# Summing a late scale and shift on VectorE, and reordering squares, constant products and weight pieces around three norms of a two-layer trunk

## The chip, the core and the metric

The kernel runs on one core of a Trainium2 chip. The metric is the device time of one execution in microseconds (us), the median of several runs; a profiled execution gives the trace. The engines are TensorE (PE in the profile; its weight loads are PEld), VectorE (DVE), ScalarE (ACT), GpSimd (POOL) and SyncE (SP, which issues the loads of weights). Each engine takes its instructions in the order in which they are written; they meet by semaphores.

## What is computed

A trunk of two layers, with 256 tokens of 1024 values in float32. Layer 0 mixes tokens by chunkwise retention and has a dense SwiGLU; layer 1 mixes by attention with forget gates against shared keys and values, and has a SwiGLU of 8 experts, two for each token. Ahead of each of these stands an RMS norm, whose scale and shift (and the gate behind) come from a product of a conditioning vector with a matrix.

```python
def reference(x, c, ada_w, ada_b, norm_g, ...):
    c_act = jax.nn.silu(c)
    h = x
    for l in range(DEPTH):                                   # DEPTH = 2, N_A = 1
        sh1, sc1, g1, sh2, sc2, g2 = jnp.split(c_act @ ada_w[l] + ada_b[l], 6, axis=-1)
        if l == N_A:
            kv_sh, kv_sc = jnp.split(c_act @ kv_ada_w + kv_ada_b, 2, axis=-1)
            hn_kv = modulate(rmsnorm(h, kv_norm_g), kv_sh, kv_sc)
            shared = fox_shared_kv(hn_kv, fox_w_kv, fox_w_f, fox_b_f)
        a = modulate(rmsnorm(h, norm_g[l, 0]), sh1, sc1)
        if l < N_A:
            mix = retention(a, ret_w_in[l], ret_w_o[l])
        else:
            mix = forgetting_attention(a, fox_w_qg[l - N_A], fox_w_o[l - N_A], *shared)
        h = h + g1[:, None, :] * mix
        m = modulate(rmsnorm(h, norm_g[l, 1]), sh2, sc2)
        ff = swiglu(m, ...) if l % 2 == 0 else moe_swiglu(m, ...)
        h = h + g2[:, None, :] * ff
    f_sh, f_sc = jnp.split(c_act @ final_ada_w + final_ada_b, 2, axis=-1)
    return modulate(rmsnorm(h, final_norm_g), f_sh, f_sc)
```

## The kernel before

The residual stream lies transposed in SBUF as `hT` (128 x 8 x 256: eight blocks of 128 features, 256 tokens). A product in float32 is made of three passes over halves: each factor is split into a high part that TensorE takes at full rate and a residue, and hi x hi, hi x lo and lo x hi are added in PSUM (`PASSES`). The high part of a weight, `whi`, is a cast on ACT (line 153); the residue `wlo` is a subtraction on DVE (recorded at line 184, or where else a list of late steps is run).

**The stream.** All weights pass through one `Stream`. An item is a block of 1 MB, `raw`, which SP loads into one of four buffers; it is worked off in two halves of 128x1024. For a weight, a half gives `whi` and `wlo`, of which six pairs exist. An item with a "use" is no weight: it is a block of a matrix whose product with the conditioning vector is wanted (a constant product). DVE multiplies its rows with the vector and sums them into a tile `adaacc` (lines 257 and 259, 128x1024); eight such steps make one of the vectors (g1, sh2, sc2, ...), and then PE transposes the sum (`pc`, line 268), ACT adds it up (line 273) and DVE adds the bias (line 275). Weights and "use" items stand mixed in one list, and `half()` hands out the next made pair, makes up to three further steps ahead (`fill`), and calls `tick()`, which lets waiting side work go on one step. So the order in which ACT and DVE get casts, residues, constant products and the rest is the order in which these calls are written and the list is laid out.

**The opening.** The first norm needs its scale and shift (sc1, sh1) before the first projection. Each comes in two halves, n = 0 and n = 1. For each half PE multiplies 16 blocks into a bank `prow` (line 306), ACT copies it (line 321), and PE turns it into a column `pcol` (line 317). The half n = 1 comes in between the first retention projections: `pa` (line 572), then `prow`, `pcol`, `pq` (line 724). `shift(n)` makes the high part `ah` (ACT) and the residue `al` (DVE) of the modulated input.

**The norms.** `out_acc` (line 588) adds the last projection of a mixer into four banks `acc`, block by block; two blocks later DVE updates `hT` (line 594) and ACT squares it (line 495), and `norm.sum` sums the squares of earlier blocks over features on PE, with one column as the result (`st`, line 501). So the `st` products stand between the `acc` products. Then `finish`: the root on ACT (`nv`), a Newton step and a diagonal `dg` on DVE, its broadcast `rb` on PE (line 520). `modulate` makes `mt` on DVE (line 529), the high part (`mh`, `kh`, `qh`) on ACT (line 532) and the residue (`ml`, `kl`, `ql`) on DVE (line 535). Norm 1 stands ahead of the SwiGLU of layer 0, norm 2 ahead of keys, values and queries of layer 1, norm 3 ahead of the experts. At norm 1 the next products are gate and up (`pg`, `pu`), 11 pieces each, at norm 2 the keys (`pk`), four pieces; the first piece takes two halves pass by pass (line 557), the others half by half (line 564). Behind norm 3 come the logits of the router, a choice of two experts per token and a gather by products (`pcum`, `P`, `pxe`, line 1227).

## Time and profile before

| what | value |
|---|---|
| median of 3 runs | 1609.03 us (1606.09 to 1609.97) |
| profiled execution, its own time | 1610.43 us |
| its span in the trace | 1608.3 us |
| mean granted clock of TensorE | 0.984 |
| PE busy | 1568.3 us |
| DVE busy | 1388.3 us |
| ACT busy | 1101.7 us |
| POOL busy | 8.7 us |

Busy times are sums over the span; an engine's idle time matters only where the engine that sets the pace waits for it. The experts fill the trace from about 640 us on. The opening, the retention, norm 1 (about 230 to 255 us), the SwiGLU, norm 2 (437 to 452 us), the attention and norm 3 (590 to 625 us) lie before.

### The profile page before, as it was taken

What the parts mean: (1) busy time and instruction counts of PE and PEld (TensorE: products, weight loads), DVE (VectorE), ACT (ScalarE), POOL (GpSimd) and SP (SyncE); (2) the same over time, 40 slices, a digit from 0 to 9 for tenths busy, and PEclk for the clock granted to TensorE, in tenths of its full rate; (3) what the DMA queues carried; (4) which work ended last, traced back from release to release, by engine and by line L of the source; (5) the groups of instructions that cost most, each with busy time, mean ns of one, the idle gap of its engine ahead of it and who ended that gap; (6) DMA issues with size and microseconds to landing.
All of it is one profiled execution on the core that took longest, in us unless ns stands there. A gap on an engine that the chain in (4) does not pass through costs nothing. (4 is left out here: it accounts for less than half of the span.)

```text
span 1608.3 us, 23189 instructions
## 1 busy us (share of the span) xinstructions
PE 1568.3 (98%) x8799; PEld 1345.0 (84%) x8799; DVE 1388.3 (86%) x1649; ACT 1101.7 (68%) x1515; POOL 8.7 (1%) x19
## 2 busy tenths in 40 slices
PE   7999999999999998999999999999999999999996
PEld 5888899999988887888888888888888888888884
DVE  3889878888797977989989989989989988988977
ACT  3444546544475758777887787888778788778774
POOL 0000000000000000000000000000000000000000
PEclk9999988999999998999999999999999999999998
DMA  9888786999868346999999999999999999999990
GB/s 357 296 308 284 288 288 223 351 334 350 301 250 287 132 140 246 372 374 375 354 342 374 351 375 379 357 342 371 351 387 369 358 343 362 357 387 361 362 369 28
DMA packets 182020, 516.02 MB, mean 321 GB/s; under 512 B 8192, under 2 KB 51504, under 8 KB 181904
## 3 DMA queue, kind: packets, MB, share of 16 engines
q1 hardware_dynamic: 180576, 510.82, 85.8%
q0 software_dynamic: 1120, 3.58, 0.6%
q8 instruction: 71, 1.16, 0.3%
q14 instruction: 45, 0.37, 0.1%
q10 hardware_dynamic: 208, 0.08, 0.0%
HBM read 513.40 MB, written 1.05 MB: 320 GB/s over the span
## 5 line engine op out<-in xcount | busy, mean ns | idle before, releaser
L184 DVE TENSOR_TENSOR wlo<-raw,whi 128x1024 fp32r<-128x1024 f32 x830 | 968.9, 1218 | 74.2 <-ACT whi L153 69.7
L153 ACT CAST whi<-raw 128x1024 fp32r<-128x1024 f32 x842 | 863.3, 1053 | 202.0 <-PE yd L572 54.4
L572 PE MATMUL pgu<-whi,xeh 128*128 128x512 f32 x896 | 354.7, 396 | 0.1
L572 PE MATMUL pgu<-wlo,xeh 128*128 128x512 f32 x896 | 349.8, 390 | 0.8 <-DVE wlo L184 0.8
L572 PE MATMUL pgu<-whi,xel 128*128 128x512 f32 x896 | 349.4, 390 | 0.0
L572 PEld LDWEIGHTS pgu<-whi,xel 128*128 128x128 f32 x896 | 168.4, 188 | 36.0
L572 PEld LDWEIGHTS pgu<-wlo,xeh 128*128 128x128 f32 x896 | 168.8, 188 | 33.9 <-DVE wlo L184 1.4
L572 PEld LDWEIGHTS pgu<-whi,xeh 128*128 128x128 f32 x896 | 168.6, 188 | 33.3 <-ACT whi L153 0.5
L572 PE MATMUL yd<-wlo,ehh 128*128 128x512 f32 x448 | 174.5, 390 | 1.2 <-DVE wlo L184 1.2
L572 PE MATMUL yd<-whi,ehh 128*128 128x512 f32 x448 | 174.4, 389 | 0.0
L572 PE MATMUL yd<-whi,ehl 128*128 128x512 f32 x448 | 174.3, 389 | 0.0
L259 DVE SCALAR_TENSOR_TENSOR adaacc<-raw,csil,adaacc 128x1024 f32<-128x1024 f32 x98 | 125.6, 1282 | 1.9
L572 PEld LDWEIGHTS yd<-wlo,ehh 128*128 128x128 f32 x448 | 84.1, 188 | 19.5 <-DVE wlo L184 2.1
L572 PEld LDWEIGHTS yd<-whi,ehh 128*128 128x128 f32 x448 | 84.1, 188 | 17.5
L572 PEld LDWEIGHTS yd<-whi,ehl 128*128 128x128 f32 x448 | 84.1, 188 | 17.4
L213 DVE TENSOR_TENSOR ehl<-pTe,ehh 128x512 fp32r<-128x512 f32 x56 | 38.7, 690 | 38.0 <-ACT ehh L212 37.9
L1315 ACT ACTIVATE ehd<-pgu 128x512 f32<-128x512 f32 x56 | 33.5, 600 | 30.9 <-PE pgu L572 30.9
L572 PE MATMUL pa<-whi,ah 128*128 128x512 f32 x128 | 50.8, 397 | 1.5 <-ACT whi L153 1.5
L212 ACT CAST ehh<-pTe 128x512 fp32r<-128x512 f32 x56 | 32.9, 587 | 28.3 <-PE pTe L1250 28.3
L572 PE MATMUL pa<-wlo,ah 128*128 128x512 f32 x128 | 50.0, 391 | 0.8 <-DVE wlo L690 0.8
L572 PE MATMUL pa<-whi,al 128*128 128x512 f32 x128 | 50.3, 393 | 0.0
L588 PE MATMUL acc<-hh,whi 128*128 128x256 f32 x176 | 49.0, 279 | 0.0
(376 smaller groups left out, 1982.9 us busy)
## 6 DMA issues: line engine op xcount, KB each, us to landing
raw<-in_moe_w_gate_dram SPq DMA_DIRECT2D x112, 1024.0 KB, 7.3
raw<-in_moe_w_up_dram SPq DMA_DIRECT2D x112, 1024.0 KB, 7.2
raw<-in_moe_w_down_dram SPq DMA_DIRECT2D x112, 1024.0 KB, 7.3
raw<-in_ada_w_dram SPq DMA_DIRECT2D x48, 1024.0 KB, 7.2
raw<-in_ret_w_in_dram SPq DMA_DIRECT2D x22, 1024.0 KB, 7.8
raw<-in_ffn_w_gate_dram SPq DMA_DIRECT2D x11, 1024.0 KB, 6.6
raw<-in_ffn_w_up_dram SPq DMA_DIRECT2D x11, 1024.0 KB, 6.9
raw<-in_ffn_w_down_dram SPq DMA_DIRECT2D x11, 1024.0 KB, 7.0
```

The lines of the kernel that those rows point to most:

```text
L153: act.copy(hi, part)
L184: f()
L212: act.copy(hi, src)
L213: vec.tensor_tensor(lo, src, hi.bitcast(F32), op=OP.subtract)
L259: vec.scalar_tensor_tensor(acc, raw[:, kt % 2, :], csil[:, kt:kt + 1], acc, op0=OP.mult, op1=OP.add)
L572: mm(dst, xs[b][:, kt0 + k, t * 128:t * 128 + 128], w[a][:, k, :], start=(first and k == 0 and i == 0), stop=(last and k == nk - 1 and i = ...
L588: mm(acc[nt // 2][:, nt % 2, :], w[a][:, k, nt % 4 * 128:nt % 4 * 128 + 128], xs[b][:, k, :], start=(first and nt % 2 == 0 and k == 0 and ...
L1315: act.activation(hd, pd, AF.Silu)
```

## The change

Five things change.

- **Opening.** The half n = 1 of scale and shift is summed by DVE into `late_acc`, eight operations of 128x512 for each, instead of 16 products on PE and a copy on ACT; the column products read that tile. `shift(0)` is made in two parts, with one step of the stream behind each, and one `prepare()` goes.
- **Constant products.** In the stretches of the list from `wr[-3]` to `wf_[1]` and from `wf_[-3]` to `wx[1]`, which are worked off around norms 1 and 2, the weights come first and the "use" items after them.
- **Squares.** GpSimd adds squares in pairs: 0 and 1; 2 and 3, then that to the first; 4 and 5. PE sums four tiles (0, 4, 6, 7) in place of eight, and all of them after the last `acc` product. Five small products into a bank `idle` are added: one ahead of the sum, two ahead of `rb`, two after it.
- **First pieces.** The first two pieces (`pg` and `pu`; keys 0 and 1) go together in `proj_b2`: four halves at once, 32 products for each of three passes. The first two calls of `half` may still make "use" steps; the ticks come after the passes.
- **Norm 3.** `out_acc` of layer 1 makes two halves of the experts' weights ahead of the norm, where before they were made behind it.

```diff
--- before.py
+++ after.py
@@ -173,13 +173,14 @@
                 steps -= 1
             return later
 
-        def half(self, steps=3):
+        def half(self, steps=3, beside=True, spare=None):
 
             while not self.made:
                 self.start()
             w = self.made.pop(0)
-            later = self.fill(self.spare, steps)
-            tick()
+            later = self.fill(self.spare if spare is None else spare, steps)
+            if beside:
+                tick()
             for f in later:
                 f()
             return w
@@ -301,7 +302,15 @@
         src, off, pitch, _ = ada_src(0, name)
 
         def use(raw, s, h):
-            if h == 0:
+            if n:
+                acc = late_acc[:, 512 * (name == "sh1"):][:, 0:512]
+                for k in (2 * h, 2 * h + 1):
+                    kt = 4 * s + k
+                    if kt == 0:
+                        vec.tensor_scalar(acc, raw[:, k, :], csil[:, 0:1], None, op0=OP.mult)
+                    else:
+                        vec.scalar_tensor_tensor(acc, raw[:, k, :], csil[:, kt:kt + 1], acc, op0=OP.mult, op1=OP.add)
+            elif h == 0:
                 for k in range(4):
                     mm(prow[32 * k:32 * k + 32, :], csp[:, 4 * s + k, :], raw[:, k, :], start=(s == 0),
                        stop=(s == 1), skip_group_check=True)
@@ -313,12 +322,14 @@
 
         bias = ada_src(0, name)[3]
         i = (8 if name == "sh1" else 0) + 4 * n
+        src = late_acc[:, 512 * (name == "sh1"):] if n else rows_sb
         for m in range(4):
-            mm(pcol[:, i + m:i + m + 1], rows_sb[:, m * 128:(m + 1) * 128], ones[:, 0:1], start=True, stop=True)
+            mm(pcol[:, i + m:i + m + 1], src[:, m * 128:(m + 1) * 128], ones[:, 0:1], start=True, stop=True)
         vec.tensor_tensor(t[:, n * 4:n * 4 + 4], pcol[:, i:i + 4], bias[:, n * 4:n * 4 + 4], op=OP.add)
 
     def first_col(name, n, t):
-        act.copy(rows_sb, prow)
+        if n == 0:
+            act.copy(rows_sb, prow)
         turn_col(name, n, t)
 
     ADA = ("sh1", "sc1", "g1", "sh2", "sc2", "g2")
@@ -441,6 +452,10 @@
         + rows(final_ada_w, 0, 2 * D, "fshift", row_bcast(final_ada_b, 0, D), 0.0, None)
         + rows(final_ada_w, D, 2 * D, "fscale", row_bcast(final_ada_b, D, D), 1.0,
                row_bcast(final_norm_g, 0, D)), 0, 70)
+    for a, b in ((wr[-3], wf_[1]), (wf_[-3], wx[1])):
+        lo, hi = (next(i for i, it in enumerate(stream.items) if it is w) for w in (a, b))
+        part = stream.items[lo:hi + 1]
+        stream.items[lo:hi + 1] = [it for it in part if "use" not in it] + [it for it in part if "use" in it]
     for i in range(16, 20):
         stream.items[i]["behind"] = i - 4
     chunks = [(e, j, min(2, EJ - j)) for e in range(NE) for j in range(0, EJ, 2)]
@@ -494,18 +509,22 @@
             sq = self.p.tile([128, S], F32, tag="mt", bufs=8, name="sq")
             act.activation(sq, hT[:, kt, :], AF.Square)
             self.sq.append(sq)
-
-        def sum(self, upto=KT):
-            while self.n < min(upto, len(self.sq)):
+            for a, b in {1: ((0, 1),), 3: ((2, 3), (0, 2)), 5: ((4, 5),)}.get(kt, ()):
+                nc.gpsimd.tensor_tensor(self.sq[a], self.sq[a], self.sq[b], op=OP.add)
+
+        def sum(self):
+            for i in (0, 4, 6, 7):
                 for t in range(TT):
-                    mm(self.st[:, t:t + 1], self.sq[self.n][:, t * 128:(t + 1) * 128], invd,
-                       start=(self.n == 0 and t == 0), stop=(self.n == KT - 1), skip_group_check=True)
-                self.n += 1
+                    mm(self.st[:, t:t + 1], self.sq[i][:, t * 128:(t + 1) * 128], invd,
+                       start=(i + t == 0), stop=(i == 7), skip_group_check=True)
 
         def finish(self, fillers=(gap, gap)):
             if self.sq:
+                busy(1)
                 self.sum()
             fillers[0]()
+            if self.sq:
+                busy(2)
             p = self.p
             v = self.v
             act.activation(v, self.st, AF.Sqrt, bias=epsc)
@@ -519,6 +538,8 @@
             self.rb = bank([128, S], name="rb", tag="at")
             mm(self.rb, ones, dg.rearrange("p t k -> p (t k)"), start=True, stop=True)
             fillers[1]()
+            if self.sq:
+                busy(2)
 
         def modulate(self, g, sh, hi, lo=None):
 
@@ -547,16 +568,20 @@
 
     PASSES = ((0, 0), (1, 0), (0, 1))
 
-    def proj_b(dst, xs, first=False):
-
-        if first:
-            w = [stream.half(), stream.half()]
-            for i, (a, b) in enumerate(PASSES):
-                for kt in range(KT):
-                    for j in range(2):
-                        mm(dst[:, j, :], w[j][a][:, kt, :], xs[b][:, kt, :], start=(kt + i + j == 0),
-                           stop=(i == 2 and kt == KT - 1), skip_group_check=True)
-            return
+    def proj_b2(dsts, xs):
+
+        w = [stream.half(3 if j < 2 else 0, False) for j in range(4)]
+        for i, (a, b) in enumerate(PASSES):
+            for kt in range(KT):
+                for j in range(4):
+                    mm(dsts[j // 2][:, j % 2, :], w[j][a][:, kt, :], xs[b][:, kt, :], start=(kt + i + j % 2 == 0),
+                       stop=(i == 2 and kt == KT - 1), skip_group_check=True)
+            tick()
+            if i:
+                tick()
+
+    def proj_b(dst, xs):
+
         for j in range(2):
             w = stream.half()
             for i, (a, b) in enumerate(PASSES):
@@ -582,7 +607,7 @@
 
         for nt in range(KT):
             if nt % 4 == 0:
-                w = stream.half(0 if last else 3)
+                w = stream.half(3) if not last else stream.half(2 if nt == 0 else 0, spare=1)
             for k in range(nk):
                 for i, (a, b) in enumerate(PASSES):
                     mm(acc[nt // 2][:, nt % 2, :], w[a][:, k, nt % 4 * 128:nt % 4 * 128 + 128], xs[b][:, k, :],
@@ -594,7 +619,6 @@
                         vec.scalar_tensor_tensor(hT[:, m, :], acc[m // 2][:, m % 2, :], gcol[:, m:m + 1],
                                                  hT[:, m, :], op0=OP.mult, op1=OP.add)
                         norm.square(m)
-                norm.sum(nt - 2)
 
     def accs():
         return [bank([128, 2, S], name=f"acc{i}") for i in range(4)]
@@ -634,6 +658,7 @@
             vec.tensor_copy(hT[:, kt:kt + 2, :], px)
         else:
             act.copy(hT[:, kt:kt + 2, :], px)
+    late_acc = ada_acc()
     prow, pcol = bank([128, 512], name="prow", tag="at"), bank([128, 16], name="pcol", tag="at")
     stream.start()
     stream.start()
@@ -660,10 +685,10 @@
                 mts.append(t)
                 vec.scalar_tensor_tensor(t, hT[:, kt, :], G[:, kt:kt + 1], rb_sb, op0=OP.mult, op1=OP.mult)
 
-        def shift(n):
-            for kt in range(n * 4, n * 4 + 4):
+        def shift(n, halves=(0, 4)):
+            for kt in range(n * 4 + halves[0], n * 4 + halves[1]):
                 act.activation(ah[:, kt, :], mts[kt], AF.Identity, bias=sh[:, kt:kt + 1])
-            for kt in range(n * 4, n * 4 + 4):
+            for kt in range(n * 4 + halves[0], n * 4 + halves[1]):
                 vec.scalar_tensor_tensor(al[:, kt, :], mts[kt], sh[:, kt:kt + 1], ah[:, kt, :].bitcast(F32),
                                          op0=OP.add, op1=OP.subtract)
 
@@ -678,7 +703,16 @@
         busy(1)
         first_col("sh1", 0, sh)
         busy(3)
-        shift(0)
+        shift(0, (0, 2))
+        los = []
+        stream.step(los)
+        for f in los:
+            f()
+        shift(0, (2, 4))
+        los = []
+        stream.step(los)
+        for f in los:
+            f()
         nc.gpsimd.tensor_copy(keeppad[:, 0:4], sh[:, 0:4])
 
         def prepare():
@@ -739,7 +773,6 @@
         pv0 = [bank([128, 512], name="pa") for _ in range(TT)]
         pg0 = [bank([128, 512], name="pa", tag="at") for _ in range(TT)]
         prepare()
-        prepare()
         tok0(pv0, 0)
         prepare()
         tok0(pg0, 0)
@@ -749,7 +782,6 @@
         qk0(pqk, 0, (0,))
         for _ in range(4):
             stream.start()
-        act.copy(rows_sb, prow)
         los = []
         stream.step(los)
         w = stream.made.pop(0)
@@ -856,11 +888,16 @@
         for j in range(NJ + 1):
             if j < NJ:
                 pg = bank([128, 2, S], name="pg", tag="at")
-                proj_b(pg, xs, j == 0)
+                if j:
+                    proj_b(pg, xs)
+                else:
+                    pu = bank([128, 2, S], name="pu", tag="at")
+                    proj_b2((pg, pu), xs)
                 hd = fp.tile([128, 2, S], F32, tag="hd", bufs=2, name="hd")
                 act.activation(hd, pg, AF.Silu)
-                pu = bank([128, 2, S], name="pu", tag="at")
-                proj_b(pu, xs)
+                if j:
+                    pu = bank([128, 2, S], name="pu", tag="at")
+                    proj_b(pu, xs)
                 vec.tensor_tensor(hd, pu, hd, op=OP.mult)
                 hh = fp.tile([128, 2, S], F32R, tag="hh", bufs=2, name="hh")
                 hl = fp.tile([128, 2, S], F32R, tag="hl", bufs=2, name="hl")
@@ -955,10 +992,14 @@
 
         kT = xp2.tile([128, KT, S], F32, name="fkT")
 
-        def keys(j):
-            pk = bank([128, 2, S], name="pk")
-            proj_b(pk, kv, j == 0)
-            act.copy(kT[:, 2 * j:2 * j + 2, :], pk)
+        def keys(js):
+            pks = [bank([128, 2, S], name="pk") for _ in js]
+            if len(js) == 2:
+                proj_b2(pks, kv)
+            else:
+                proj_b(pks[0], kv)
+            for j, pk in zip(js, pks):
+                act.copy(kT[:, 2 * j:2 * j + 2, :], pk)
 
         def queries(j):
             pk = bank([128, 2, S], name="pk")
@@ -1056,12 +1097,11 @@
             yield
 
         side.append(early())
-        keys(0)
+        keys((0, 1))
         split(wfh, wfl, wf)
-        keys(1)
-        keys(2)
+        keys((2,))
         side.append(forget())
-        keys(3)
+        keys((3,))
         vv = xp2.tile([128, TT, D], F32, name="vv")
         values(0)
         values(1)
```

On ACT behind norm 1: `sq` are the squares, `mh` the modulated input, `pc` the sums of a constant product, `hd` and `hh` the first piece of the SwiGLU. Before:

```order
L495 ACTIVATE sq<-hT 128x256 x8
L511 ACTIVATE nv<-st,epsc 128x2
L532 ACTIVATE mh<-mt,ada_sh_0_1235 128x256 x8
L153 CAST whi<-raw 128x1024 x2
L273 ACTIVATE pc,ada_g_0_2424<-pc 128x128 x8
L153 CAST whi<-raw 128x1024 x2
L861 ACT_TABLE_LOAD
L861 ACTIVATE hd<-pg 128x512
```

After:

```order
L510 ACTIVATE sq<-hT 128x256 x8
L530 ACTIVATE nv<-st,epsc 128x2
L553 ACTIVATE mh<-mt,ada_sh_0_1234 128x256 x8
L274 ACTIVATE pc,ada_g_0_2442<-pc 128x128 x8
L274 ACTIVATE pc,ada_kvsh<-pc 128x128 x8
L897 ACT_TABLE_LOAD
L897 ACTIVATE hd<-pg 128x512
L213 CAST hh<-hd 128x512
L153 CAST whi<-raw 128x1024 x5
```

The four casts that stood between `mh` and the table load stand ahead of the norm; the next ones come behind `hh`.

On ACT behind norm 2: `kh` and `qh` are the inputs of keys and queries, `fkT` a finished piece of keys, `wfh` the high part of the gate's weight. Before:

```order
L532 ACTIVATE kh<-mt,ada_kvsh 128x256 x8
L153 CAST whi<-raw 128x1024 x2
L273 ACTIVATE pc,ada_g_1_4784<-pc 128x128 x8
L153 CAST whi<-raw 128x1024 x2
L532 ACTIVATE qh<-mt,ada_sh_1_2991 128x256 x8
L961 COPY fkT<-pk 128x512
L212 CAST wfh<-wf 128x128
L153 CAST whi<-raw 128x1024 x2
```

After:

```order
L553 ACTIVATE kh<-mt,ada_kvsh 128x256 x8
L274 ACTIVATE pc,ada_g_1_4825<-pc 128x128 x8
L553 ACTIVATE qh<-mt,ada_sh_1_2996 128x256 x8
L274 ACTIVATE pc,ada_sh_1_4922<-pc 128x128 x8
L1002 COPY fkT<-pk 128x512 x2
L213 CAST wfh<-wf 128x128
L153 CAST whi<-raw 128x1024 x4
```

The casts of new weights move behind `qh`, a second set of `pc` and two pieces of keys.

On DVE behind norm 2: `kl` and `ql` are residues of the inputs, `mt` the scaled inputs, `g2row` a row of a constant product. Before:

```order
L535 SCALAR_TENSOR_TENSOR kl<-mt,ada_kvsh,kh 128x256 x8
L529 SCALAR_TENSOR_TENSOR mt<-hT,G_4715,rb 128x256 x8
L184 TENSOR_TENSOR wlo<-raw,whi 128x1024 x2
L257 TENSOR_SCALAR adaacc<-raw,csil 128x1024
L275 TENSOR_TENSOR ada_g_1_4784<-ada_g_1_4784,vcol 128x8
```

After:

```order
L556 SCALAR_TENSOR_TENSOR kl<-mt,ada_kvsh,kh 128x256 x8
L260 SCALAR_TENSOR_TENSOR adaacc<-raw,csil,adaacc 128x1024 x6
L550 SCALAR_TENSOR_TENSOR mt<-hT,G_4724,rb 128x256 x8
L276 TENSOR_TENSOR ada_g_1_4825<-ada_g_1_4825,vcol 128x8
L556 SCALAR_TENSOR_TENSOR ql<-mt,ada_sh_1_2996,qh 128x256 x3
L276 TENSOR_TENSOR ada_sh_1_4922<-ada_sh_1_4922,vcol 128x8
L290 SCALAR_TENSOR_TENSOR g2row<-pr,rowb 128x512 x2
```

Six steps of constant products stand between `kl` and the second `mt`, and the next `wlo` stands further down.

## Rows read from the trace of the kernel before

**Rows 1.** The page, busy us with share of the span and instructions
```profile
PE 1568.3 (98%) x8799; PEld 1345.0 (84%) x8799; DVE 1388.3 (86%) x1649; ACT 1101.7 (68%) x1515; POOL 8.7 (1%) x19
```

**Rows 2.** Waits of PE to 640 us: us in total, times, longest
```profile
PE st L501 <- ACT sq L495: 2.4, 4, 1.4
...
PE pf L917 <- ACT fT L911: 1.4, 1, 1.4
```

**Rows 3.** Stretches of half clock: us, PE PEld DVE ACT POOL busy, PEclk, DMA
```profile
233.00:253.70 20.70, 19.58 (x90) 18.48 (x90) 9.82 (x30) 8.55 (x22) 0.00 (x0) 0.51 0.19 67
441.40:448.30 6.90, 5.78 (x24) 5.06 (x25) 5.74 (x15) 5.22 (x11) 0.00 (x0) 0.51 0.01 2
612.20:615.50 3.30, 2.90 (x12) 2.64 (x12) 3.30 (x7) 1.29 (x4) 0.00 (x0) 0.50 0.00 0
```

**Rows 4.** Timeline, opening, DVE and PE: start, us, engine, line, operation, [idle before]
```profile
25.64 6.90 DVE L690 TENSOR_TENSOR wlo<-raw,whi 128x1024 fp32r<-128x1024 f32 x6 [0.45 <-ACT whi L153]
...
44.40 1.92 PE L306 MATMUL prow<-raw,adaacc 128*32 128x512 f32 x16
...
47.78 0.95 PE L317 MATMUL pcol<-cm,adaacc 128*128 128x1 f32 x8
...
52.38 0.85 PE L724 MATMUL pq<-ah,wlo 128*128 128x256 f32 x5 [1.26 <-DVE wlo L762]
```

**Rows 5.** Timeline of DVE and ACT, norm 1
```profile
229.04 2.60 DVE L259 SCALAR_TENSOR_TENSOR adaacc<-raw,csil,adaacc 128x1024 f32<-128x1024 f32 x2
...
250.25 3.25 DVE L535 SCALAR_TENSOR_TENSOR ml<-mt,ada_sh,mh 128x256 fp32r<-128x256 f32 x8
...
257.69 1.28 ACT L861 ACT_TABLE_LOAD   x1
...
265.26 0.68 DVE L864 TENSOR_TENSOR hd<-pu,hd 128x512 f32<-128x512 f32 x1
```

**Rows 6.** Groups of DVE, 100 to 760 us: busy us, mean ns, idle before
```profile
L594 DVE SCALAR_TENSOR_TENSOR hT<-acc,ada_g,hT 128x256 f32<-128x256 f32 x24 | 10.3, 478 | 16.1 <-PE acc L588 16.1
```

**Rows 7.** Timeline of PE, norm 1 and the first pieces of the SwiGLU
```profile
230.90 0.28 PE L588 MATMUL acc<-z,whi 128*128 128x256 f32 x1
232.54 0.61 PE L501 MATMUL st<-invd,sq 128*128 128x1 f32 x4 [1.36 <-ACT sq L495]
...
248.19 3.78 PE L557 MATMUL pg<-mh,whi 128*128 128x256 f32 x16 [1.12 <-ACT mh L532]
...
268.51 1.17 PE L564 MATMUL pu<-mh,whi 128*128 128x256 f32 x8
...
274.04 0.28 PE L588 MATMUL acc<-hh,whi 128*128 128x256 f32 x1
```

**Rows 8.** Timeline of PE, norm 2 and the keys
```profile
432.55 0.61 PE L501 MATMUL st<-invd,sq 128*128 128x1 f32 x4 [0.60 <-ACT sq L495]
...
437.26 0.95 PE L501 MATMUL st<-invd,sq 128*128 128x1 f32 x8
...
439.36 1.07 PE L268 MATMUL pc<-cm,adaacc 128*128 128x128 f32 x8
...
443.64 3.79 PE L557 MATMUL pk<-kh,whi 128*128 128x256 f32 x16 [1.12 <-ACT kh L532]
...
464.84 1.07 PE L908 MATMUL pfT<-kh,wfh 128*16 128x256 f32 x8
```

**Rows 9.** ACT's busy time by `pc` (window), then timeline of DVE and ACT, norm 2
```profile
448.00:451.20 3.20, 2.84 (x16) 0.96 0.00 0
...
448.87 3.22 DVE L529 SCALAR_TENSOR_TENSOR mt<-hT,G,rb 128x256 f32<-128x256 f32 x8
...
456.22 0.58 ACT L961 COPY fkT<-pk 128x512 f32<-128x512 f32 x1
```

**Rows 10.** Timeline, norm 3, DVE and PE
```profile
613.75 3.48 DVE L1176 TENSOR_TENSOR wlo<-raw,whi 128x1024 fp32r<-128x1024 f32 x3
...
617.45 0.71 PE L1227 MATMUL pxe<-P,mth 128*128 128x256 f32 x4 [1.97 <-DVE cmax L1179]
```

## The prediction

> **What bounds the kernel now.** I read the page's totals first: TensorE (PE) is busy 98% of the span of 1608.3 us [rows 1], so a saving counts only where PE waits or runs at its low clock. I then took PE's waits by releaser, the granted clock by stretch, and the order of work on PE, ScalarE (ACT) and VectorE (DVE) around the three inner norms. PE's waits are few and short; the sum of squares waits 2.4 us in all, four times [rows 2]. What the waits hide is the clock: after the pauses around a norm PE is granted 0.5 of full speed (1.2 of 2.4 GHz), for 20.7 us at norm 1, 6.9 us at norm 2 and in pieces like the one of 3.3 us at norm 3 [rows 3]. These 31 us go at half rate, and the rest of PE's work is dense. The reader should see in each group which work PE does next, and whether that work needs ACT or DVE to be through a queue first.
>
> **Opening.** The late half of scale and shift was summed by 16 PE products of 32x512 twice, 1.92 us each; after the second, PE goes on to the shift column, and then waits 1.26 us for a residue `wlo` of line 762 [rows 4]. The change puts the two sums on DVE: eight operations of 128x512 each. No row shows that shape; half of an adaacc of 128x1024 (2.60 us for two) is 0.65 us [rows 5], so a sum takes about 5.2 us. DVE starts the first when its six opening residues are through, at 32.5 [rows 4], and ends near 38; the second, behind the column and four `mt` of the shape of the residual update (0.478 each [rows 6], a little less back to back), ends at about 46.5. PE no longer has 3.8 us of products, but it reaches the shift column at about 43 and waits there for DVE until 46.5, where before it came at 47.78 [rows 4]. The chain behind (ah, al, wlo) is unchanged, so PE's dense stretch begins 1.0 to 1.3 us earlier, at best. A pause of 3.5 us may cost a piece of half clock, as the one at norm 3 did (3.3 us at 0.50 [rows 3], so 1.6 us lost). I take -0.5; ends -1.3 and +1.
>
> **Sum of squares and clock at norm 1.** Before, four groups of `st` products stood between the last `acc` groups. At 231.18 PE came to the first and waited 1.36 us for a square (DVE had two adaacc ahead of its residual updates), the clock fell, and the rest of the groups, the `st`, the broadcast `rb` and the first `pg` ran at half rate until 253.7 [rows 3, 7]. After, the `acc` groups come in one piece and the adaacc are behind the norm. The 24 matmuls that were left at 231.18 take 0.115 us each (48 of that shape in 5.53 us, 268.51 to 274.04 [rows 7]), 2.75 us, less about 0.9 for eight transpositions that move behind the norm (1.07 by the `pc` row [rows 8]): the last `acc` ends near 233.0. From there to the end of `st` norm 2 takes 2.1 us (437.26 to 439.36 [rows 8]); I take 2.3 for the GpSimd sum. From the end of `st` to the first projection norm 2 has 4.3 us (439.36 to 443.64 [rows 8]), some 0.45 of it `rb` at half clock, so 3.8. The projection starts at 239.1 instead of 248.19 [rows 7]: **-9.1 us**. For that the `idle` fillers must hold the clock. They are five small products, and they lie in time in which PE waited anyway: one while the last squares are made, two for the chain to `rb`, two for `mh` or `kh`, where PE waited 1.12 us [rows 8].
>
> **What comes after it at norm 1.** This is the part that gives the gain back. Before, ACT cast new weights two at a time between its other steps. Now four halves are ready and 96 matmuls run dense, 11.0 us, but no weight cast is issued until ACT is through mh, two sets of eight `pc`, the table load, `hd` and `hh`. Count from the first projection matmul. DVE ends `ml` at 5.3 (253.5 against 248.19 [rows 5, 7]), then does six adaacc, one of them the cheaper first product, 7.2 us, to 12.5. The second set of `pc` waits for PE's transposes behind the 96 matmuls, at 11.9; a set takes 2.9 us [rows 9], so 14.8; table load 1.28, `hd` 0.6 (as `fkT` of the same shape [rows 9]), DVE's product 0.68 [rows 5], `hh` 0.6: 18.0; the first new `whi`, 1 us, at 19.1. PE has stood since 11.9, so 7.2 us. Its `wlo` is behind `hl` (0.69), two adaacc (2.6) and its own 1.22: 22.6, another 2.4 us of waiting, 0.9 for the piece's whi pass taken off; a later `wlo` is behind two more adaacc, 0.9 us. The second `pu` piece ends at 32.6, against 25.85 before (274.04 less 248.19 [rows 7]): **+6.75**. Two waits of that length will let the clock fall; each fall before lasted 3.3 us or more, a loss of 1.6, partly inside waits: I take +1.75 (0 to 3.4). Norm 1 in all: -9.1 + 6.75 + 1.75 = **-0.6** (-3 to +2).
>
> **Norm 2** has less to win and the same to lose. Eight `st` columns take 0.95 us [rows 8]; sixteen of them between the groups are 1.9 at most, 1.4 as they overlap with the products behind. A wait of 0.60 for a square in their midst [rows 8] goes too. With the tail 0.2 longer and `rb` 0.45 shorter the projection starts 2.3 us earlier. Again from its first matmul: DVE ends `kl` at 5.3 and, where it used to do `mt` for the queries at once (at 448.87, 5.2 behind 443.64 [rows 8, 9]), it has six adaacc, 7.7 us, first. So `qh` on ACT ends at 16.7 (it follows each `mt`), and only behind it come eight `pc` (2.9), two `fkT` (0.58 each [rows 9]) and `wfh` (0.3): 21.0, then the first new `whi`, 22.1. PE, through with 96 matmuls, the transposes and `pr` at about 14.8, waits 7.2 us. The residue `wlo` stands behind the last `pc`'s addition, `g2row`, `wfl` and two adaacc: 24.9, a wait of 1.9. The third keys piece ends at 29.6 against 21.2 before (464.84 less 443.64 [rows 8]): +8.4. With -2.3 for the start, +1.1 for a clock that falls again, and -1.4 for a wait that was there (`pf` for `fT` [rows 2]) and that will now be covered, norm 2 is **+5.8** (+3 to +8).
>
> **Norm 3.** Two expert halves move ahead of the norm, behind the last work of the attention on DVE. DVE's `wlo` x3 of 3.48 us in front of `cmax` becomes one, and the 1.97 us for which PE waited on `cmax` (it frees the bank of `pcum`) goes [rows 10]. The `st` in one piece save 1.4 as at norm 2, less 0.3 of tail; other pauses of the routing stay, and its clock with them. -1.97 - 1.4 + 0.3 = **-3.1** (-1.5 to -4.5).
>
> **GpSimd's sum.** Before, GpSimd is busy 8.7 us in the whole span, with 19 instructions [rows 1], and none of them is an add of 128x256. The nearest row is DVE's update of that shape, 0.478 us [rows 6]; the lower end is that, the upper end four times it, 1.9. I take 0.8, since two operands of SBUF are no less work than DVE's. Three adds stand behind the fourth square, and two pairs of updates and squares follow it by at least 1.8 us, so 2.4 us of adds put `st` some 0.2 to 0.5 us behind the squares.
>
> The Trainium skill, page "GPSIMD Engine Reference", section 3.1, puts an elementwise add at 4497 ns against 2293 on DVE, 1.96 times. By that an add here is an estimated 0.94 us, and the sum would be 0.4 us later per norm, 1.2 us in all; no row here shows it.
>
> **The sum.** -0.5 - 0.6 + 5.8 - 3.1 = +1.6 us. The profiled execution took 1610.4 us (span 1608.3 and 2.1 around it), so 1612.0; the median of the runs is 1609.0, and against it the forecast is 1610.6. About 0.3% (4.8 us) is what a measurement of this kernel can tell from no change. From the ends of the parts, not all reached at once, this case spans 1606 to 1616.
>
> **Rivals.** First, *the new casts arrive in time, and the starts are kept*. If the queues on ACT and DVE drain about 4 us faster at each of norms 1 and 2 than I stack them (`hd` or `fkT` not behind a late set of `pc`), the waits halve and the sum is about +1.6 - 8 = -6.4: 1602.6. For it: mh and kh are paced by DVE's `mt`, and a dense clock brings all forward. Against: every step I stacked stands ahead of the cast on an engine that takes its queue in order.
>
> Second, slower, *GpSimd's adds set the end of the sum*. It decides from about 1.1 us per add, where 3.3 us of adds pass the 1.8 us and the tail I allowed. At 1.9 us each of three norms waits 3 us longer, and the clock falls before the projection, some 2 us more at norm 1: +1.6 + 11 = 1621.6; at 1.3 us some 1614. For it: no row bounds the add from above. Against: it is far from the nearest row.
>
> Third, *the clock falls in norm 1 all the same*, because one filler does not cover the wait for the last squares. Then about 8 us of chain and projection go at half rate: +4, 1614.6.
>
> **How the numbers follow.** The sum as worked out 0.50; casts in time 0.22; GpSimd late 0.13; the clock falls 0.15. Faster by over 0.3%: the first rival nearly whole (0.20) and a tenth and a half of the forecast (0.07), 0.27. Slower: GpSimd late 0.09, the clock 0.08 and a fifth of the forecast 0.10, 0.27. The rest, 0.46, within. The range leaves out the slow end of GpSimd and the quickest casts: 1602 to 1618.
>
> **What would show it.** PE's first `pg`+`pu` matmul near 239 at clock 1.00; a wait of about 7 us of PE on ACT's `whi` behind the 96 matmuls of norms 1 and 2, and one of about 2 us on `wlo`; no wait on `cmax`; GpSimd adds near 0.8 us. Without the two 7 us waits the forecast is wrong on the fast side; adds over 1.1 us or a wait of `st` on GpSimd of more than 1 us make it wrong on the slow side.

## The result: 8.5 us slower, and the profile after

The changed kernel takes 1617.49 us (median of 5 runs, 1616.47 to 1618.32) against 1609.03: 1.0057 times the time before, 95% interval 1.0039 to 1.0075. The time lies in the range, 0.5 us from its slow end; the forecast of no change (within 0.3%) is wrong, since it is slower by 0.57%. The span of the profiled execution grows by 7.4 us, from 1608.3 to 1615.7 [rows 1], and PE's mean granted clock is 0.985 against 0.984. The page's totals after, as busy time, share of the span and instructions of each engine:

```profile
PE 1565.6 (97%) x8749; PEld 1343.4 (83%) x8749; DVE 1400.4 (87%) x1665; ACT 1101.0 (68%) x1513; POOL 17.3 (1%) x31
```

PE has less work than before and a longer span, so it waits more. Its waits up to 660 us (engine, line, what it waited for: total, times, longest), to be read against [rows 2]:

```profile
PE pg L589 <- ACT whi L153: 6.9, 1, 6.9
PE pcol L327 <- DVE adaacc L312: 3.6, 2, 2.3
PE pk L589 <- ACT whi L153: 3.6, 1, 3.6
...
PE pr L289 <- DVE mt L550: 1.9, 1, 1.9
PE pu L577 <- DVE mt L550: 1.7, 1, 1.7
...
PE pg L589 <- DVE wlo L192: 1.4, 1, 1.4
...
PE pk L589 <- DVE wlo L192: 1.0, 1, 1.0
...
PE st L518 <- POOL sq L513: 0.5, 2, 0.3
```

The waits that went are those of `st` for the squares, of `pf` for `fT` and of `pxe` for `cmax`. New are the waits for casts and residues of weights and for `mt` at norms 1 and 2, and those of `pcol` for DVE's sums in the opening. Where the time came and went is seen from the start of the same PE work in both traces:

| first PE work of a stretch | before | after | stretch changed by |
|---|---|---|---|
| `pq`, behind the opening | 52.38 | 52.23 | -0.15 |
| `pg`, behind norm 1 | 248.19 | 239.38 | -8.7 |
| `acc` out product, two pieces of `pg`, `pu` done | 274.04 | 277.98 | +12.8 |
| `pk`, behind norm 2 | 443.64 | 447.43 | -0.15 |
| `pf`, keys done | 474.59 | 487.40 | +9.0 |
| `pgu`, behind norm 3 | 620.68 | 629.07 | -4.4 |
| end of the span | 1608.3 | 1615.7 | -1.0 |

PE around norm 1, after (start, duration, what, and in brackets the idle time before it and who ended it; a filler `idle` is two matmuls in the trace), against [rows 7]:

```profile
232.70 0.59 PE L567 MATMUL idle<-cm 128*128 128x256 f32 x2
233.47 2.19 PE L518 MATMUL st<-invd,sq 128*128 128x1 f32 x16 [0.17 <-POOL sq L513]
...
239.38 0.50 PE L577 MATMUL pg<-mh,whi 128*128 128x256 f32 x2 [0.32 <-ACT mh L553]
241.58 0.80 PE L577 MATMUL pu<-mh,whi 128*128 128x256 f32 x2 [1.70 <-DVE mt L550]
...
253.81 1.03 PE L269 MATMUL pc<-cm,adaacc 128*128 128x128 f32 x8
261.76 2.08 PE L589 MATMUL pg<-mh,whi 128*128 128x256 f32 x8 [6.91 <-ACT whi L153]
265.20 2.08 PE L589 MATMUL pg<-mh,wlo 128*128 128x256 f32 x8 [1.36 <-DVE wlo L192]
```

ACT in the same stretch:

```profile
254.45 0.26 ACT L274 ACTIVATE pc<-pc 128x128 f32<-128x128 f32 x1 [9.37 <-PE pc L269]
...
257.50 1.28 ACT L897 ACT_TABLE_LOAD   x1
258.79 0.60 ACT L897 ACTIVATE hd<-pg 128x512 f32<-128x512 f32 x1
260.15 0.62 ACT L213 CAST hh<-hd 128x512 fp32r<-128x512 f32 x1 [0.76 <-DVE hd L901]
260.67 3.88 ACT L153 CAST whi<-raw 128x1024 fp32r<-128x1024 f32 x4
```

ACT stands idle for 9.37 us while PE runs the first two pieces: the next thing in its queue is the set of `pc`, which needs PE's transposes, and these stand behind the 96 products. Only then come table load, `hd`, `hh` and the first cast, and PE waits 6.91 us for it. PE at norm 2, after, against [rows 8]:

```profile
442.20 1.51 PE L269 MATMUL pc<-cm,adaacc 128*128 128x128 f32 x8
443.50 1.92 PE L567 MATMUL idle<-cm 128*128 128x256 f32 x4
445.20 1.04 PE L539 MATMUL rb<-dg,cm 128*128 128x256 f32 x2
...
447.43 4.04 PE L577 MATMUL pk<-kh,whi 128*128 128x256 f32 x32 [0.32 <-ACT kh L553]
...
460.69 1.10 PE L289 MATMUL pr<-adaacc,cm 128*128 128x512 f32 x2 [0.95 <-DVE adaacc L260]
463.74 2.08 PE L289 MATMUL pr<-adaacc,cm 128*128 128x512 f32 x2 [1.95 <-DVE mt L550]
469.39 2.08 PE L589 MATMUL pk<-kh,whi 128*128 128x256 f32 x8 [3.58 <-ACT whi L153]
472.48 2.08 PE L589 MATMUL pk<-kh,wlo 128*128 128x256 f32 x8 [1.01 <-DVE wlo L192]
```

DVE has `dg` for `rb` ready at 444.06, and ACT reaches the first new cast at norm 2 without an idle moment in front of it:

```profile
443.58 0.48 DVE L537 TENSOR_SCALAR dg<-cm,nr 128x128 f32<-128x128 f32 x2
```

```profile
468.27 3.90 ACT L153 CAST whi<-raw 128x1024 fp32r<-128x1024 f32 x4
```

Behind the waits the clock is low again. Busy time by stretch (PE, PEld, DVE, ACT, POOL, then granted clock, DMA share, GB/s), against [rows 3]:

```profile
241.50:244.70 3.20, 3.12 (x14) 3.12 (x15) 3.20 (x10) 3.02 (x16) 0.00 (x0) 0.50 0.00 0
261.70:268.70 7.00, 5.58 (x24) 5.29 (x25) 6.93 (x7) 2.85 (x4) 0.00 (x0) 0.51 0.51 176
443.50:445.20 1.70, 1.70 (x5) 1.35 (x5) 0.68 (x5) 0.00 (x0) 0.00 (x0) 0.50 0.10 36
463.00:476.00 13.00, 7.67 (x26) 5.81 (x27) 10.61 (x18) 8.98 (x27) 0.53 (x1) 0.51 0.54 181
```

### The profile page after: what moved, and what is told of

Its sections match the earlier page's. It is cut to its first block, busy times and chain, and to the rows that moved or that the text cites. A ratio compares the mean times of both kernels' runs of the same rounds, so it can differ in the third digit from the quotient of the medians.

```text
span 1615.7 us, 23138 instructions
## 1 busy us (share of the span) xinstructions
PE 1565.6 (97%) x8749; PEld 1343.4 (83%) x8749; DVE 1400.4 (87%) x1665; ACT 1101.0 (68%) x1513; POOL 17.3 (1%) x31
## 3 DMA queue, kind: packets, MB, share of 16 engines
q0 software_dynamic: 1120, 3.58, 0.6%
## 5 line engine op out<-in xcount | busy, mean ns | idle before, releaser
L214 DVE TENSOR_TENSOR ehl<-pTe,ehh 128x512 fp32r<-128x512 f32 x56 | 38.7, 691 | 38.0 <-ACT ehh L213 37.8
L213 ACT CAST ehh<-pTe 128x512 fp32r<-128x512 f32 x56 | 32.9, 587 | 28.3 <-PE pTe L1290 28.3
```

The source lines that it names most:

```text
L213: act.copy(hi, src)
L214: vec.tensor_tensor(lo, src, hi.bitcast(F32), op=OP.subtract)
```

## The experiments

Each ratio is against the kernel before, measured on the same chip, with its 95% interval. The theory to be tested is the prediction's: constant products behind the weights, together with two first pieces at once, leave the next casts at the end of the queues. Its rival is that one of the two alone does it, or something beside them: the fillers, the opening or the two halves made ahead.

**First pieces one at a time again** (constant products stay behind the weights):

```diff
-                    proj_b2((pg, pu), xs)
+                proj_b(pg, xs, j == 0)
...
-        keys((0, 1))
+        keys((0,))
         split(wfh, wfl, wf)
+        keys((1,))
```

> The changed kernel with one part undone: the first weight pieces go one by one again, as before. Theory S (new casts stand too far back in ACT's and DVE's queues behind norms 1 and 2, because the first two pieces issue none): the wait of PE on whi of 6.9 us at norm 1 falls below 2 us and the one of 3.6 us at norm 2 below 2 us; the SwiGLU's first out product starts 3 to 5 us earlier than the changed kernel's 277.98, the pf transposition 6 to 9 us earlier than 487.40; time 1608 to 1611. Rival C (the loss is the clock and the wait for a bank ahead of and inside the first projection, the casts only show it): the first projection starts as in the changed kernel, the out product comes within 2 us of it; time 1614 or more.

Measured 1610.05 us, 1.0014 [0.9998, 1.0031]: about 7 us less than the change as a whole. The waits at norm 1 shrink to 1.8 and 1.0. At norm 2, where the expectation said below 2, a wait for `whi` of 3.92 us stays, and its cause is another. ACT's row, then SyncE's loads of weight blocks (the rows in which they are issued):

```profile
456.73 2.00 ACT L153 CAST whi<-raw 128x1024 fp32r<-128x1024 f32 x2 [6.36 <-DMA raw<-in_fox_w_kv_dram]
```

```profile
421.68 6.57 SPq L132 DMA_DIRECT2D raw<-in_ada_w_dram  x2
431.00 0.37 SPq L132 DMA_DIRECT2D raw<-in_final_ada_w_dram  x1
451.63 0.37 SPq L132 DMA_DIRECT2D raw<-in_fox_w_kv_dram  x1
```

The cast waits for a load. With the weights first in the list, the last four loads ahead of the norm (416.60 to 431.00) are of constant products; they hold the four `raw` buffers when the norm comes, and DVE works them off only behind it; so no weight block is issued until 451.63. Before, a weight block stood between them:

```profile
427.07 0.37 SPq L132 DMA_DIRECT2D raw<-in_fox_w_kv_dram  x1
431.67 0.37 SPq L132 DMA_DIRECT2D raw<-in_final_ada_w_dram  x1
454.38 0.37 SPq L132 DMA_DIRECT2D raw<-in_fox_w_kv_dram  x1
```

**Constant products between the weights again** (the two first pieces stay together):

```diff
-    for a, b in ((wr[-3], wf_[1]), (wf_[-3], wx[1])):
-        lo, hi = ...
-        part = stream.items[lo:hi + 1]
-        stream.items[lo:hi + 1] = ...
```

> The changed kernel with one part undone: constant products stand among the weights again around norms 1 and 2; the first two pieces still go at once. Theory S: two casts follow mh and kh on ACT, so the waits on whi behind the first two pieces fall by more than half, but constant products stand before the norms again; the pf transposition 4 to 8 us earlier than 487.40, time 1609 to 1613. Rival C: nothing changes behind the norms but the order, time 1615 or more.

Measured 1612.46 us, 1.0034 [1.0017, 1.0051]. The waits for `whi` are gone, but `pf` starts only 2.0 us earlier than in the changed kernel (485.39), not 4 to 8. In their place `pr` waits 6.00 us at norm 2 for the `mt` of the queries, which stand on DVE behind four steps of constant products and two `wlo`. By the code `pr` doesn't read `mt`; it takes a bank of the same four as `rb`, which `mt` reads:

```profile
465.60 2.07 PE L289 MATMUL pr<-adaacc,cm 128*128 128x512 f32 x2 [6.00 <-DVE mt L546]
```

**Both undone** (opening, squares, halves made ahead stay):

```diff
-    for a, b in ((wr[-3], wf_[1]), (wf_[-3], wx[1])):
...
-                    proj_b2((pg, pu), xs)
+                proj_b(pg, xs, j == 0)
```

> The changed kernel with both undone, the first two pieces at once and the constant products behind the weights; opening, squares on GpSimd with fillers, and the expert halves ahead of norm 3 stay. Theory L (at the norms all four raw buffers hold blocks of constant products when these stand behind the weights, so no weight can be loaded until DVE has freed one; casts late in ACT's queue come on top): no wait of PE on whi behind norm 1 or 2 of over 0.5 us; the first projection of norm 1 falls back to 246 to 248 because the two constant products stand ahead of the residual update again; pf transposition within 3 us of before's 474.59, first expert product 617 to 620; time 1604 to 1608. Rival C (squares, fillers and clock cost what was lost): first expert product not before 623, time 1611 or more.

Measured 1601.7 us, 0.9965 [0.995, 0.9979], faster than expected. No wait for a weight is left behind norms 1 and 2. So the two parts cost 15.8 us together, where undoing one gives 7.4 and undoing the other 5.0; the rest of the change is a gain. Alone, the constant products cost 8.4 us (1610.05 against 1601.7) and the pieces 10.8 (1612.46 against 1601.7): the costs overlap, by 3.3 us, about as much as the intervals tell apart. The four combinations, all else as in the changed kernel, with two stretches of PE from start to start (us):

| constant products behind | two pieces at once | us | `pg` to out product | `pk` to `pf` |
|---|---|---|---|---|
| yes | yes (after) | 1617.49 | 38.6 | 40.0 |
| yes | no | 1610.05 | 31.3 | 37.8 |
| no | yes | 1612.46 | 28.3 | 35.1 |
| no | no | 1601.7 | 24.0 | 28.6 |

The stretches leave out what the order wins ahead of norm 1: in the order of the rows, the first `pg` starts at 239.38, 241.36, 248.37 and 245.67.

**Constant products behind at norm 1 alone**, pieces one at a time:

```diff
-    for a, b in ((wr[-3], wf_[1]), (wf_[-3], wx[1])):
+    for a, b in ((wr[-3], wf_[1]),):
```

> The changed kernel with the first pieces one by one and the constant products behind the weights at norm 1 only. Theory L: norm 1 as in the run e1 (out product near 272.6, some waits on whi stay), norm 2 without the waits on whi of 3.9 and 1.1 us that e1 had, since a weight block lies loaded: pf transposition 471 to 475, first expert product 615 to 618; time 1602 to 1606, faster than before. Rival C: norm 2 is no better than in e1 (pf at 478), time 1609 or more.

Measured 1604.83 us, 0.9983 [0.9969, 0.9996]: the first `pg` comes at 239.42 as in the changed kernel, but `pg` and `pu` wait 1.4 and 1.5 us for `whi`. At norm 2 no wait for a weight is left: a weight block's load is issued at 432.57 there, and not at 451.63 as in the run with both norms reordered, which speaks for the full buffers as the cause of that wait. Against both undone (span 1601.8 and 1598.4) there is no gain in it.

**One more weight block ahead of the constant products**, and two more casts right behind the norm:

```diff
-    for a, b in ((wr[-3], wf_[1]), (wf_[-3], wx[1])):
+    for a, b in ((wr[-3], wf_[2]), (wf_[-3], wx[2])):
...
-        w = [stream.half(3 if j < 2 else 0, False) for j in range(4)]
+        w = [stream.half(steps[j], False) for j in range(4)]
```

with `steps` (3, 6, 3, 1) for `pg`, `pu` and (1, 1, 0, 0) for the keys.

> The changed kernel with one more 1 MB weight ahead of the constant products at norms 1 and 2, so that two further halves are cast behind mh and kh, and with the constant products' steps put where DVE waits at norm 1 and behind the queries' mt at norm 2. Theory S: no wait on whi of over 2.5 us behind the first two pieces of either norm; the out product starts 6 to 8 us earlier than 277.98, the pf transposition 11 to 15 us earlier than 487.40; time 1602 to 1606, faster than the kernel before. Rival C: as those waits only take up what the half clock and the bank wait cost, under 4 us are won, time 1613 or more.

Measured 1610.82 us, 1.0016 [0.9999, 1.0033]; the expectation missed. At norm 1 the wait for `whi` is gone, and the out product comes at 273.41, not 277.98, although the first `pg` starts 3.7 us later (243.06); so the cast's place in ACT's queue was the cause of the wait there. At norm 2 the wait has only moved to the load. ACT, then PE:

```profile
468.32 1.99 ACT L153 CAST whi<-raw 128x1024 fp32r<-128x1024 f32 x2 [8.72 <-DMA raw<-in_fox_w_kv_dram]
```

```profile
469.41 2.07 PE L589 MATMUL pk<-kh,whi 128*128 128x256 f32 x8 [7.73 <-ACT whi L153]
```

**The changed kernel without the five fillers:**

```diff
             if self.sq:
-                busy(1)
                 self.sum()
             fillers[0]()
-            if self.sq:
-                busy(2)
```

and the same behind `rb`.

> The changed kernel without the five idle products at each of the three norms. Theory S: the waits on whi are unchanged within 1 us; the first projection of norm 2 starts 1 us earlier than the changed kernel's 447.43, because the fillers ran at half clock ahead of rb there, that of norm 1 within 1.5 us of 239.38; time within 2 us of the changed kernel. Rival C, one way: without fillers the clock is at half rate through the first projection of norm 1 and the time grows by 4 us or more; the other way: the fillers themselves are the cost and the time falls by 4 us or more.

Measured 1617.7 us, 1.0069 [1.0045, 1.0093]: the same as with them. By stretches they help and hurt. Without them the out product at norm 1 comes 1.06 us later (279.04), but `pk` 0.5 us earlier (446.92): from the last `acc` product to `pk` norm 2 takes 7.4 us in place of 8.3.

**The opening as before**, in the kernel with constant products behind at norm 1 alone:

```diff
-            if n:
-                acc = late_acc[:, 512 * (name == "sh1"):][:, 0:512]
...
-            elif h == 0:
+            if h == 0:
...
-        shift(0, (0, 2))
...
+        shift(0)
```

> The run e7 with the opening as before too (late scale and shift on TensorE). From the traces of before and after, in which the dense stretch after the opening begins at 52.38 and 52.23: within 0.7 us of e7, so the same by a timing; if the sum on DVE delays other work there, 1 us or more faster than e7.

Measured 1603.94 us, 0.9977 [0.9962, 0.9993], against 0.9983 with the new opening. The difference is within the intervals: the opening is worth nothing that can be measured.

**The kernel before with the halves made ahead** (only the line in `out_acc` and the argument it needs):

```diff
-                w = stream.half(0 if last else 3)
+                w = stream.half(3) if not last else stream.half(2 if nt == 0 else 0, spare=1)
```

> The kernel before with one part of the change alone: two expert halves made ahead of norm 3. My prediction's step: the wait on cmax of 1.97 us goes and the first expert product starts 2 to 3 us earlier than 620.68, time 1605 to 1607. Rival: DVE or ACT is late for the squares instead, or the clock falls elsewhere, and the first expert product stays within 1 us of 620.68, time as before.

Measured 1615.27 us, 1.0049 [1.0034, 1.0063]; the expectation missed, and it shows a mistake of mine in reading the diff. The line applies to the last `out_acc` ahead of each of the three norms, not of norm 3 alone. At norm 3 it does what it should: `pxe` doesn't wait for `cmax`. At norms 1 and 2 the two extra steps are also halves of weights: two casts on ACT and two residues `wlo` (2.35 us) on DVE, ahead of the residual updates, so the squares come late and `st` waits. DVE at norm 1 before, then DVE and PE in this run:

```profile
231.55 1.66 DVE L594 SCALAR_TENSOR_TENSOR hT<-acc,ada_g,hT 128x256 f32<-128x256 f32 x4
```

```profile
231.59 2.35 DVE L184 TENSOR_TENSOR wlo<-raw,whi 128x1024 fp32r<-128x1024 f32 x2
233.86 1.65 DVE L594 SCALAR_TENSOR_TENSOR hT<-acc,ada_g,hT 128x256 f32<-128x256 f32 x4
```

```profile
234.84 1.01 PE L501 MATMUL st<-invd,sq 128*128 128x1 f32 x4 [3.68 <-ACT sq L495]
...
437.32 1.01 PE L501 MATMUL st<-invd,sq 128*128 128x1 f32 x4 [3.96 <-ACT sq L495]
```

**The same for norm 3 alone**, in the kernel before (`ahead` is true for layer 1's `out_acc` only):

```diff
+                w = stream.half(3) if not last else stream.half(2 if ahead and nt == 0 else 0, spare=1)
```

> The kernel before with two expert halves made ahead of norm 3 and nothing else changed (e8 had also added steps ahead of norms 1 and 2). If my step in the prediction holds: norms 1 and 2 as before within 0.5 us, the wait on cmax of 1.97 us goes, the first expert product 2 to 3 us before 620.68, time 1605 to 1606. If e8 was slow for norm 3 itself: slower than before.

Measured 1607.45 us, 0.999 [0.9967, 1.0014]: the wait for `cmax` is gone, and the gain is too small to be told from none. Its norm 1 is the code of the kernel before, and yet the out product starts at 272.15, not 274.04: two traces of the same code differ by 1.9 us there, as the clock falls later in this one (0.80 from 232 to 236 us, where before it was 0.65).

**The squares alone**, in the kernel before: GpSimd's adds, one sum behind the last `acc`, the fillers.

```diff
+            for a, b in {1: ((0, 1),), 3: ((2, 3), (0, 2)), 5: ((4, 5),)}.get(kt, ()):
+                nc.gpsimd.tensor_tensor(self.sq[a], self.sq[a], self.sq[b], op=OP.add)
...
+            for i in (0, 4, 6, 7):
...
-                norm.sum(nt - 2)
```

> The kernel before with the squares alone changed: added in pairs on GpSimd (0.75 us each in the trace of the changed kernel), summed in one piece, with the idle products. My prediction's steps: 16 st columns fewer and no st wait among the groups, so norm 1's first projection 3 to 7 us before 248.19 (the two constant products stay ahead of the residual update), norms 2 and 3 1.5 to 2 us shorter; time 1600 to 1604. Rival: GpSimd's adds delay the sum by what the fewer columns save, time 1606 or more.

Measured 1602.51 us, 0.9963 [0.9943, 0.9983]. This part alone gives what the kernel with both orders undone gives. (The run keeps GpSimd's adds, the sum in one piece and the fillers together; which of the first two gives the gain isn't shown. The fillers don't, by the last run below.) Out product at 268.91 instead of 274.04, `pf` at 468.52 instead of 474.59: the gain is made at norm 1, where the half clock, 20.7 us long before [rows 3], is now about 7 (stretches of 4 us at 0.76, 0.50 and 0.89 lack 3.4 us of full clock, so 6.8 us of half):

```profile
236.00:240.00 4.00, 3.39 (x21) 3.31 (x22) 0.56 (x4) 0.88 (x3) 1.16 (x2) 0.76 0.39 157
240.00:244.00 4.00, 4.00 (x13) 3.37 (x12) 1.25 (x6) 0.00 (x0) 0.00 (x0) 0.50 0.00 0
244.00:248.00 4.00, 4.00 (x21) 3.11 (x21) 4.00 (x12) 3.85 (x9) 0.00 (x0) 0.89 0.00 0
```

**Both orders undone, the halves ahead at norm 3 alone:**

```diff
-                w = stream.half(3) if not last else stream.half(2 if nt == 0 else 0, spare=1)
+                w = stream.half(3) if not last else stream.half(2 if ahead and nt == 0 else 0, spare=1)
```

> The run e6 with the two extra stream steps of the last output projection kept at norm 3 only; at norms 1 and 2 none, as before. Theory L extended (these two steps put constant products ahead of the residual update at norms 1 and 2 when the list is mixed; e6 and e8 show waits of st of 2.2 and 3.7 to 4.0 us there): the waits of st on GpSimd fall from 2.2 us each to under 1, the first projection of norm 1 starts near 243 and that of norm 2 2 to 3 us earlier relative to norm 1; time 1597 to 1600. Rival: the weights made ahead by these steps are missed behind the norms, waits on whi appear, time 1601 or more.

Measured 1600.49 us, 0.9944 [0.9922, 0.9966]; just above the range expected. `st` waits 1.1 us in all for GpSimd's sum instead of 4.4, which moves the time less than the intervals tell apart. What the two steps put ahead of the updates is again two `wlo` (at 231.09 in the trace with both orders undone), and not constant products, as the expectation has it: two of those stand there in this run too.

**The same without fillers:**

```diff
-                busy(1)
...
-                busy(2)
```

> The run e10 without the idle products. If the fillers hold the clock at the norms: half clock in more of the stretch from the last acc product to the first projections, time 1 to 4 us above e10. If they are empty, as in e4: within 1 us of e10.

Measured 1598.14 us, 0.9935 [0.9914, 0.9956]. It is 0.65% faster than the kernel before and 1.2% faster than the changed one, and again not distinguishable from the same kernel with fillers. The expectation missed: the time is 2.4 us below the run with fillers, neither 1 to 4 above it nor within 1. The fillers do hold the clock; norm 1 with them and without:

```profile
236.00:240.00 4.00, 3.93 (x25) 3.84 (x26) 1.18 (x8) 0.26 (x1) 0.50 (x1) 0.71 0.23 95
240.00:244.00 4.00, 3.68 (x16) 2.72 (x15) 2.05 (x7) 1.44 (x4) 0.00 (x0) 0.87 0.00 0
244.00:248.00 4.00, 4.00 (x29) 3.48 (x29) 4.00 (x12) 4.00 (x9) 0.00 (x0) 1.00 0.00 0
```

```profile
236.00:240.00 4.00, 3.93 (x22) 3.51 (x21) 1.27 (x8) 0.26 (x1) 0.06 (x1) 0.61 0.11 45
240.00:244.00 4.00, 2.82 (x9) 2.10 (x10) 2.73 (x7) 2.21 (x6) 0.00 (x0) 0.50 0.00 0
244.00:248.00 4.00, 4.00 (x24) 4.00 (x24) 4.00 (x11) 3.94 (x11) 0.00 (x0) 0.61 0.00 0
```

Yet the out product starts at 267.10 with them and at 267.36 without: `pg` starts 0.8 us earlier without them (242.35 for 243.12), and from there to the out product the low clock costs 1.0 us (25.0 against 24.0).

## Why the prediction was right and wrong, by its own steps

The mechanism was right: a start won at norm 1, given back by casts that come late, and a loss at norm 2. The sum to `pgu` came to +8.4 (629.07 less 620.68) where the steps gave +1.6. Norm 1 was put too low by 4.7 and norm 2 by 3.1, the opening by 0.35; norm 3 was better by 1.3 than said.

- **Opening**, -0.5: -0.15. DVE's sums cost more than was estimated (the first takes 6.0 us, from 32.34 to 38.34, in place of 5.2), and PE's pause turned into two waits of `pcol`, 1.34 and 2.25 us.
- **Start of norm 1**, -9.1: -8.7 (`pg` at 239.38, where 239.1 was said).
- **What comes after it at norm 1**, +8.5 with the clock: +12.8. *This is the first step that failed.* I took the 96 products as dense, 11.0 us; they took 14.4 (239.38 to 253.81). After two products PE waits 1.70 us for the last `mt` before `pu`. Its operand is not late, since `pg` has used the same block of `mh`; what `mt` frees is the bank in which `rb` lay, and `pu`, which now comes at once, needs it. That the bank is the cause is read from rows and code; no run changed it alone. Two things speak for it: at norm 2 two pieces also go at once, but their banks are of another set than `rb`'s, and `pk` has no such wait; and `pr`, which shares `rb`'s set and doesn't read `mt`, waits for `mt` there (1.95 us). Behind the wait the clock is 0.50 until 244.7; of the 3.4 us that the products took too long, the wait is 1.7 and the low clock the rest.

  The stack of ACT behind it was right, only 3.3 us later: the first cast reaches PE 22.4 us after `pg`, not 19.1, and the waits are 6.91 and 1.36 (7.2 and 2.4 predicted; the 0.9 for a later `wlo` is named in the prediction but not in its 32.6, and no such wait came). Of the 4.3 us that this part was put too low, 3.4 are the 96 products; behind the cast, 5.58 us of PE's work at 0.51 of the clock cost some 2.7 us where 1.75 were put down, and a set of transposes stands ahead of the out product (0.8 us).
- **Norm 2**, +5.8: +8.9. The second step that failed is its start, -2.3 put down and -0.15 found. Up to the last `acc` product PE wins 1.9 us (2.0 put down); the tail behind it loses them. The sum in one piece ends 3.0 us behind that product, 2.2 before (0.2 more was put down, 0.8 found), and from there to `pk` it takes 5.2 us, 4.3 before. The `dg` for `rb` is ready at 444.06, but the fillers, at 0.50 of the clock, hold PE until 445.20; I had costed them at nothing because they lay in waiting time. The run without fillers takes 4.4 us for that last part, so 0.8 is theirs.

  Behind the start it is +9.0 for +8.1. The cast reaches PE 22.0 us after the first `pk` (22.1 said), but PE came to it late: `pr` waited 0.95 and 1.95 us, which the prediction doesn't have, so the cast's wait was 3.58 and not 7.2, and the residue's 1.01. The low clock cost more than the 1.1 put down: 7.67 us of PE's work at 0.51 from 463 to 476 us took some 3.8 us longer. So the missing second wait of 7 us was no sign of a fast result, as the prediction took it to be. Not in the prediction at all are the full `raw` buffers, which came out when the queue was mended.
- **Norm 3**, -3.1: -4.4, of which 0.4 lies in the attention. The wait for `cmax` went as said. From the start of the last products into `acc` (570.29 and 582.69) to `pgu`, 50.4 us become 46.4; the halves alone take 1.8 off (48.6), the squares alone 0.7 (49.7), differences that two traces of the same code can show too. Why both together take 4.0 stays open.
- **GpSimd's add**, 0.8 us: 0.73 on average, and `st` waits 0.3 at most for it in the changed kernel. That rival falls.
- **Rivals.** The casts did not come in time. The clock fell in norm 1, the third rival, but behind the start and not in the sum, and for another reason.

The direction hung on a sum near zero of terms of 6 to 9 us each; an error of 4.7 us in the largest decided it. And I read the halves made ahead as a change of norm 3 only; it is one of all three norms, though in the changed kernel this costs little (`st` waits 0.5 us in all).

## What to carry to other kernels

When a reordering wins a start, write out the whole queue of the engine that feeds the next work, and also what lies in the loading buffers: a block that is used late holds the place of one that is wanted early. Taking items of two kinds apart in an in-order stream loses the mixing that kept both supplied. Of a change with several parts, one part (here the squares, -0.37%) may carry all the gain, and the costs of two others may overlap (8.4 and 10.8 us alone, 15.8 together), so that undoing only one wins back less than it costs alone.

## What the runs showed of the hardware

GpSimd's add of 128x256 in float32 takes 0.73 us (mean of twelve), 1.5 times VectorE's update of that shape [rows 6]. The Trainium skill, page "GPSIMD Engine Reference", section 3.1, has a ratio of 1.96 for an elementwise add of 2048 values. The measured ratio is lower, but the update is another operation than an add, and no run here times VectorE's add of that shape. Unexpected was that the fillers kept a granted clock of 0.87 to 1.00 where without them it was 0.50 to 0.61 for 8 us, and won nothing: they delay the first projection by 0.8 us, about the 1.0 us that the clock gives back, and at norm 2 of the changed kernel fillers that themselves ran at 0.50 of the clock held the broadcast `rb` back for 1.1 us after its operand was ready.
